# A two-layer decoder on one core: rows of split activations at other offsets and pitches, and products of weight groups in four orders

## The chip, the core and the metric

The kernel runs on one core of one Trainium2 chip. The metric is the device time of one execution in microseconds (us); less is better. A core has five engines with instruction queues of their own: TensorE (PE, matrix products; the load of the stationary weights is shown apart as PEld), VectorE (DVE), ScalarE (ACT), GpSimd (POOL) and SyncE (SP, used here to issue DMA transfers). They work on SBUF, a memory of 128 partitions; TensorE writes to PSUM, and VectorE and ScalarE read from there.

## The reference

A sequence of 16 learned prefix tokens and 256 input tokens (272 in all, model width 2048, 16 heads) goes through two layers. Layer 0 has attention with a forget gate, layer 1 stick-breaking attention against a K/V projection that is computed once. Each layer ends with an MLP that squares the positive part. Cut to what matters:

```python
def squared_relu_mlp(h, w_up, w_down):
    u = h @ w_up
    return jnp.square(jax.nn.relu(u)) @ w_down
...
        if layer < N_A_LAYERS:
            proj = a @ fox_w_in[i]
            q, k, v, f_logit = jnp.split(proj, [D_MODEL, 2 * D_MODEL, 3 * D_MODEL], axis=-1)
...
            o = forgetting_attention(split_heads(q), split_heads(k), split_heads(v), cum_logf)
            h = h + o.reshape(b, length, D_MODEL) @ fox_w_o[i]
        else:
            c = rms_norm(h, kv_norm)
            k_s, v_s = jnp.split(c @ w_kv, 2, axis=-1)
...
            q = split_heads(a @ sb_w_q[i])
            o = stick_breaking_attention(q, shared_k, shared_v)
            h = h + o.reshape(b, length, D_MODEL) @ sb_w_o[i]
        h = h + squared_relu_mlp(rms_norm(h, norm_mlp[layer]), w_up[layer], w_down[layer])
    return rms_norm(h, final_norm)[:, N_META:]
```

All of it is float32. The hidden width of the MLP is 8192.

## The kernel before

Activations are kept with features on the partitions: 16 chunks of 128 features, each with a row of 272 tokens (256 in layer 1, which needs no prefix queries). To have nearly float32 exactness at the rate of a shorter format, each operand x is split into a high part and a low part, both of the type float32r, and a product w·x is the sum of three: high·high, high·low and low·high.

**Rows.** The class `Split` holds one stage's activations. A tile has, for each of the 16 chunks, a row of XROW = 576 elements; the high half begins at element XHI = 16, the low half right behind it. `both` is the view over the two halves of a row together. Two such tiles exist and are used in turn (tag "x"). The stages and their labels: a0 (input of layer 0's q, k, v), o0 (attention output), m0 (input of the MLP), u0_0 to u0_3 (the four quarters of the MLP's hidden vector), a1 and kv (inputs of layer 1's q and of K/V), o1, m1, u1_0 to u1_3. The last one, `ob`, takes the output. The helpers `split_chunk`, `put_split` and the evacuation in `mlp` write the halves with ScalarE (high) and VectorE (low).

**Groups.** All projections go through `gemm_group`, one call for 512 output features. There are 96 calls, numbered by u = 1 to 96: 12 for q, k and v of layer 0 (a0), 4 on o0, 32 in its MLP (16 on m0, 4 on each of u0_0 to u0_3), 4 for q of layer 1 (a1), 8 for K/V (kv), 4 on o1 and 32 in the MLP (m1, u1_0 to u1_3). A call walks over the 2048 input features in four blocks kb of four chunks kc. For each block, two DMA transfers on SP's queue bring 512 KB each into tiles `raw` (ring of four), and each half is split: ScalarE writes `whi` (line 213), VectorE `wlo` (line 214), with rings of four tiles each, so two blocks are held. Four PSUM accumulators, m = 0 to 3, take 128 output features each.

**Order of the products.** Blocks 0 and 3 are walked output by output (m outside, all four chunks inside). Blocks 1 and 2 are walked in halves of two chunks, with all four m inside each. In layer 0 and for K/V a chunk and an m give three products of 272 columns, issued one behind the other: high weights × high half, high weights × low half, low weights × high half. In layer 1 (`pairs`) there are two: high weights × `both` (512 columns, so that the two sums stand side by side in PSUM) and low weights × high half (256 columns); in a run all products of the first kind go before those of the second. All are issued through the helper `gemm_matmul` (line 172), which pins each product behind the one before it, apart from the first group (`load_x`), where the planner of the framework may reorder. In block 3 the accumulator m is evacuated as soon as its products are issued.

Between groups, attention runs with its own products on TensorE; its exponentials and masks lie on ScalarE and VectorE beside the next group's products. `gate_products` multiplies the rows of a0 with a narrow weight block (32 columns) within the first group.

**Scratch.** `kernel` creates the program with the default size of the SBUF region kept for descriptors of dynamic DMA transfers.

## Time and profile before

| what | value |
|---|---|
| median of 2 runs | 2333.88 us (2332.91 to 2334.85) |
| profiled execution | 2332.09 us, span of its instructions 2330.3 us |
| PE busy | 2319.3 us, 16486 products |
| DVE, ACT, POOL busy | 1350.6, 1064.8 and 38.9 us |
| granted TensorE clock | 0.998 of full speed |
| read from HBM | 407.29 MB, 176 GB/s over the span |

The span is the time from the first to the last instruction of one profiled execution. Products on TensorE are pipelined: one starts while the one before it still drains, so the mean time of one product in a row of the profile is longer than the distance from its start to the next start. In a row of the table of groups stand the line, engine and operation, output <- inputs by the program's names, the shape of the stationary block and of the moving rows, the count, the busy time, the mean time of one in ns, and the idle time before with what ended it. In the timeline stand the start in us, the length of the merged stretch, and the same names.

### The profile page before, as it was taken

To read this page: it belongs to the slowest core of one execution; us is meant where nothing else is said; L and a number is where in the kernel's file an instruction comes from. 1 tells how busy PE (TensorE), PEld (TensorE's weight loads), DVE (VectorE), ACT (ScalarE), POOL (GpSimd) and SP (SyncE) were. 2 spreads that over 40 slices of the span, in tenths; PEclk is the share of its full clock that TensorE was granted. 3 is DMA by queue.
4 is the path that set the end of the run, shared out by engine and by line. 5 is a ranking of instruction groups with operands and counts; after the bars stand their busy time and mean duration, and the time that the engine had idled before them with its cause. 6 is when DMAs were issued, how large, how long until landed. Compare 5 with 4: busy or idle time off the path is not lost.

```text
span 2330.3 us, 39954 instructions
## 1 busy us (share of the span) xinstructions
PE 2319.3 (100%) x16486; PEld 2200.1 (94%) x16486; DVE 1350.6 (58%) x1923; ACT 1064.8 (46%) x1477; POOL 38.9 (2%) x58
## 2 busy tenths in 40 slices
PE   9999999999999999999999999999999999999998
PEld 9999999999999999999998999988888888888887
DVE  7665555654454455445566555566665665655665
ACT  6434344543344344334455444455543543543553
POOL 1000000000000000000000000000000000000000
PEclk9999999999999999999999999999999999999999
DMA  6544545455545555555556444446556556555553
GB/s 233 172 155 163 169 158 171 166 185 173 180 168 185 176 174 180 172 182 172 181 175 198 160 145 145 145 163 199 184 190 198 186 187 199 185 191 195 185 198 128
DMA packets 116630, 412.00 MB, mean 177 GB/s; under 512 B 13264, under 2 KB 16736, under 8 KB 116448
## 3 DMA queue, kind: packets, MB, share of 16 engines
q1 hardware_dynamic: 114560, 406.29, 52.4%
q10 hardware_dynamic: 1888, 3.16, 0.4%
q8 instruction: 129, 2.11, 0.4%
q14 instruction: 53, 0.43, 0.1%
HBM read 407.29 MB, written 2.11 MB: 176 GB/s over the span
## 4 chain that ended last, share of the span: by engine, by line
PE 99%; DVE 0%; ACT 0%; issue 0%; DVEq 0%; ACTq 0%
PE acc L172 96%; PE ps L402 0%; PE pza L581 0%; PE pv L335 0%; PE po L464 0%; PE po L620 0%; PE idle L60 0%; PE pzb L582 0%; PE po L621 0%; PE po L465 0%; PE po L622 0%; DVE ob L676 0%; PE pf L301 0%; PE pf L302 0%; PE pta L597 0%; PE pta L596 0%
## 5 line engine op out<-in xcount | busy, mean ns | idle before, releaser
L214 DVE TENSOR_TENSOR wlo<-raw,whi 128x1024 fp32r<-128x1024 f32 (+1 forms) x773 | 931.7, 1217 | 752.6 <-ACT whi L213 751.7
L213 ACT ACTIVATE whi<-raw 128x1024 fp32r<-128x1024 f32 (+1 forms) x773 | 799.2, 1050 | 960.4 <-PE acc L172 939.9
L172 PE MATMUL acc<-x_u,whi 128*128 128x272 f32 (+2 forms) x3088 | 650.8, 322 | 0.0
L172 PE MATMUL acc<-x_m,whi 128*128 128x272 f32 (+1 forms) x3072 | 649.2, 323 | 0.0
L172 PEld LDWEIGHTS acc<-x_u,whi 128*128 128x128 f32 x3088 | 497.4, 188 | 26.3
L172 PEld LDWEIGHTS acc<-x_m,whi 128*128 128x128 f32 x3072 | 495.5, 188 | 26.9
L172 PE MATMUL acc<-x_u,wlo 128*128 128x272 f32 (+1 forms) x2048 | 441.7, 280 | 0.0
L172 PE MATMUL acc<-x_m,wlo 128*128 128x272 f32 (+1 forms) x2048 | 439.4, 280 | 0.0
L172 PE MATMUL acc<-x_a,whi 128*128 128x272 f32 (+1 forms) x1792 | 363.0, 307 | 0.0
L172 PEld LDWEIGHTS acc<-x_u,wlo 128*128 128x128 f32 x2048 | 339.5, 188 | 15.9
L172 PEld LDWEIGHTS acc<-x_m,wlo 128*128 128x128 f32 x2048 | 338.5, 188 | 16.1
L172 PEld LDWEIGHTS acc<-x_a,whi 128*128 128x128 f32 x1792 | 283.5, 188 | 9.3 <-issue 0.7
L172 PE MATMUL acc<-x_a,wlo 128*128 128x272 f32 (+1 forms) x1024 | 252.9, 284 | 0.0
L172 PE MATMUL acc<-x_kv,whi 128*128 128x272 f32 x1024 | 195.8, 289 | 0.0
L172 PEld LDWEIGHTS acc<-x_a,wlo 128*128 128x128 f32 x1024 | 179.3, 188 | 4.7 <-issue 0.5
L172 PE MATMUL acc<-x_o,whi 128*128 128x272 f32 (+1 forms) x768 | 163.1, 323 | 0.0
L172 PEld LDWEIGHTS acc<-x_kv,whi 128*128 128x128 f32 x1024 | 159.9, 188 | 0.4
L172 PE MATMUL acc<-x_kv,wlo 128*128 128x272 f32 x512 | 145.9, 285 | 0.0
L252 DVE TENSOR_TENSOR hT<-acc,hT 128x256 f32<-128x256 f32 (+1 forms) x239 | 102.5, 429 | 72.0 <-PE acc L172 70.3
L172 PEld LDWEIGHTS acc<-x_o,whi 128*128 128x128 f32 x768 | 124.0, 188 | 6.7
L172 PE MATMUL acc<-x_o,wlo 128*128 128x272 f32 (+1 forms) x512 | 110.8, 282 | 0.0
L172 PEld LDWEIGHTS acc<-x_kv,wlo 128*128 128x128 f32 x512 | 96.2, 188 | 0.1
(226 smaller groups left out, 1038.5 us busy)
## 6 DMA issues: line engine op xcount, KB each, us to landing
raw<-w_up SPq DMA_DIRECT2D x256, 512.0 KB, 4.7
raw<-w_dn SPq DMA_DIRECT2D x256, 512.0 KB, 4.8
raw<-w_qkv SPq DMA_DIRECT2D x92, 512.0 KB, 4.1
raw<-w_o SPq DMA_DIRECT2D x64, 512.0 KB, 4.5
raw<-w_kv SPq DMA_DIRECT2D x64, 512.0 KB, 3.9
raw<-w_q SPq DMA_DIRECT2D x32, 512.0 KB, 4.7
fk<-f_dram ACTq DMA_DIRECT2D x4, 544.0 KB, 5.4
raw<-w_qkv SPq DMA_DIRECT2D x7, 256.0 KB, 4.7
```

What stands on the lines that cost most here:

```text
L172: ins = nc.tensor.matmul(*args, **kw).ins
L213: on_act = nc.scalar.activation(hp, src, AF.Copy)
L214: on_dve = nc.vector.tensor_tensor(out=lp, in0=src, in1=hp.bitcast(F32), op=ALU.subtract)
L252: nc.vector.tensor_tensor(out=hT[:, c, t0:], in0=a, in1=hT[:, c, t0:], op=ALU.add)
```

## The change

Three things change.

1. `Split` takes offset and pitch from a table `ROWS` by the stage's label: pitch of a row, start of the high half, start of the low half, in elements. The tile is 16 × 640 + 64 elements for every stage. In layer 1, where `both` is used, the low half still stands right behind the high half.
2. `gemm_group` chooses one of four orders by u modulo 4. The first group's first block and, for all groups, the order of m in blocks 0 and 3 stay as they are; within them, and in blocks 1 and 2, the products of a chunk and an m may be drawn apart. `kinds` lists the products (0 = high weights, 1 = low weights).
   - Without pairs: order 0 walks halves of two chunks, and in each all high × high, then all high × low, then all low × high; order 1 the same over the whole block; order 2 is the order of before; order 3 walks halves, and in each output by output the three kinds one after the other over its chunks.
   - With pairs: order 0 is the order of before; order 1 walks the whole block at once; order 2 halves, output by output; order 3 output by output over the whole block, as blocks 0 and 3.
3. The program keeps 1,024 bytes for descriptors of dynamic DMA transfers.

```diff
-XROW = 576
-XHI = 16
+ROWS = {"a0": (576, 16, 288), "kv": (640, 0, 320), "o0": (640, 16, 336), "m0": (640, 32, 352), "u0_0": (640, 48, 368),
+        "u0_1": (544, 0, 272), "u0_2": (576, 48, 320), "u0_3": (576, 0, 272),
+        "a1": (576, 0, 256), "o1": (576, 32, 288), "m1": (512, 0, 256), "u1_0": (576, 48, 304), "u1_1": (544, 16, 272),
+        "u1_2": (576, 0, 256), "u1_3": (576, 8, 264)}
+XROW = 640
...
-            rows = xs.tile([P, NC, XROW], F32R, tag="x", name=f"x_{label}")
-            self.hi, self.lo = rows[:, :, XHI:XHI + n], rows[:, :, XHI + n:XHI + 2 * n]
-            self.both = rows[:, :, XHI:XHI + 2 * n]
+            rows = xs.tile([P, NC * XROW + 64], F32R, tag="x", name=f"x_{label}")
+            pitch, hi, lo = ROWS[label]
+            rows = rows[:, hi:hi + NC * pitch].rearrange("p (c t) -> p c t", c=NC)
+            self.hi, self.lo = rows[:, :, :n], rows[:, :, lo - hi:lo - hi + n]
+            self.both = rows[:, :, :2 * n] if lo == hi + n else None
...
+            way = u % 4
             if load_x is not None and kb == 0:
                 runs = [([kc], range(4)) for kc in range(4)]
-            elif kb in (0, 3):
+            elif kb in (0, 3) or way == 3 and pairs:
                 runs = [(range(4), [m]) for m in range(4)]
+            elif way == 1:
+                runs = [(range(4), range(4))]
+            elif way == 2 and pairs:
+                runs = [(range(2 * hf, 2 * hf + 2), [m]) for hf in range(2) for m in range(4)]
             else:
                 runs = [(range(2 * hf, 2 * hf + 2), range(4)) for hf in range(2)]
             pinned[0] = load_x is None
             for kcs, ms in runs:
                 paired = [m for m in ms if pairs and m not in apart]
...
+                for some in (paired, [m for m in ms if m not in paired]):
+
+                    kinds = ([(0, sp.both, 2 * n), (1, sp.hi, n)] if some is paired else
+                             [(0, sp.hi, n), (0, sp.lo, n), (1, sp.hi, n)])
+                    if not pairs and way == 2:
+                        todo = [(i, kc, m) for m in some for kc in kcs for i in range(len(kinds))]
+                    elif not pairs and way == 3:
+                        todo = [(i, kc, m) for m in some for i in range(len(kinds)) for kc in kcs]
+                    else:
+                        todo = [(i, kc, m) for i in range(len(kinds)) for kc in kcs for m in some]
+                    for i, kc, m in todo:
+                        w, xk, cols = kinds[i]
+                        gemm_matmul(accs[m][:, :cols], parts[kc // 2][w][:, kc % 2, m * P:(m + 1) * P],
+                                    xk[:, 4 * kb + kc], start=kb == kc == i == 0,
+                                    stop=kb == kc == 3 and i == len(kinds) - 1)
...
-    ob = xs.tile([P, NC, XROW], F32, tag="x", name="ob")
+    ob = xs.tile([P, NC * XROW + 64], F32, tag="x", name="ob")[:, :NC * XROW].rearrange("p (c t) -> p c t", c=NC)
...
-    nc = bacc.Bacc("TRN2", target_bir_lowering=False, num_devices=1)
+    nc = bacc.Bacc("TRN2", target_bir_lowering=False, num_devices=1, dynamic_dma_scratch_size=1024)
```

More of the change, by code (lines that the diff above doesn't have):

```diff
@@ L229, in gemm_group @@
                 paired = [m for m in ms if pairs and m not in apart]
-                single = [m for m in ms if m not in paired]
-                for kc in kcs:
-                    for m in paired:
-                        gemm_matmul(accs[m], parts[kc // 2][0][:, kc % 2, m * P:(m + 1) * P], sp.both[:, 4 * kb + kc],
-                                    start=kb == kc == 0, stop=False)
-                for kc in kcs:
-                    for m in paired:
-                        gemm_matmul(accs[m][:, :n], parts[kc // 2][1][:, kc % 2, m * P:(m + 1) * P],
-                                    sp.hi[:, 4 * kb + kc], start=False, stop=kb == kc == 3)
-                for m in single:
-                    for kc in kcs:
-                        wh, wl = (w[:, kc % 2, m * P:(m + 1) * P] for w in parts[kc // 2])
-                        hi, lo = sp.hi[:, 4 * kb + kc], sp.lo[:, 4 * kb + kc]
-                        gemm_matmul(accs[m][:, :n], wh, hi, start=kb == kc == 0, stop=False)
-                        gemm_matmul(accs[m][:, :n], wh, lo, start=False, stop=False)
-                        gemm_matmul(accs[m][:, :n], wl, hi, start=False, stop=kb == kc == 3)
+                for some in (paired, [m for m in ms if m not in paired]):
[12 more added lines that the diff above has]
+                                    stop=kb == kc == 3 and i == len(kinds) - 1)
                 if kb == 3:
```

## The prediction, made before the result was known

> **What bounds the kernel now.** I read the page first: shares, granted clock, chain, costliest groups.

> ```profile
> span 2330.3 us, 39954 instructions
> ...
> PE 2319.3 (100%) x16486; PEld 2200.1 (94%) x16486; DVE 1350.6 (58%) x1923; ACT 1064.8 (46%) x1477; POOL 38.9 (2%) x58
> ...
> PEclk9999999999999999999999999999999999999999
> ...
> PE 99%; DVE 0%; ACT 0%; issue 0%; DVEq 0%; ACTq 0%
> PE acc L172 96%; PE ps L402 0%; PE pza L581 0%; PE pv L335 0%; PE po L464 0%; PE po L620 0%; PE idle L60 0%; PE pzb L582 0%; PE po L621 0%; PE po L465 0%; PE po L622 0%; DVE ob L676 0%; PE pf L301 0%; PE pf L302 0%; PE pta L597 0%; PE pta L596 0%
> ...
> L214 DVE TENSOR_TENSOR wlo<-raw,whi 128x1024 fp32r<-128x1024 f32 (+1 forms) x773 | 931.7, 1217 | 752.6 <-ACT whi L213 751.7
> L213 ACT ACTIVATE whi<-raw 128x1024 fp32r<-128x1024 f32 (+1 forms) x773 | 799.2, 1050 | 960.4 <-PE acc L172 939.9
> ```

> TensorE runs from end to end at the full granted clock, and 96% of the chain is the one helper line that issues the products of the groups. ScalarE, which splits the weights, stands idle for 940 us because TensorE has not yet freed a weight tile: the weights are early, not late. Next I asked what TensorE itself waits for. The whole answer is three rows, 2.6 us in all:

> ```profile
> PE pr_fin L665 <- DVE fin L659: 1.3, 1, 1.3
> PE idle L60 <- DVE mean_w L56: 1.1, 1, 1.1
> PE pms_fin L633 <- ACT sq_fin L645: 0.2, 1, 0.2
> ```

> So the time is the number of products times the distance between their starts, and the change keeps the number. Only that distance can move it. Third view: TensorE's groups by shape (count, union of their spans, mean time of one).

> ```profile
> L172 PE MATMUL acc<-x_m,whi 128*128 128x272 f32 x2048 | 382.7, 288 | 0.0
> ...
> L172 PE MATMUL acc<-x_u,wlo 128*128 128x272 f32 x1024 | 289.8, 283 | 0.0
> L172 PE MATMUL acc<-x_m,whi 128*128 128x512 f32 x1024 | 266.5, 392 | 0.0
> ...
> L172 PE MATMUL acc<-x_m,wlo 128*128 128x256 f32 x1024 | 149.5, 278 | 0.0
> ...
> L598 PE MATMUL pta<-eh,nones_r 128*128 128x288 f32 x8 | 2.4, 296 | 0.0
> ```

> Products overlap, so a mean is longer than the distance. The distances come from the timeline of TensorE; first an MLP stage of layer 0 (start, time, what, count):

> ```profile
> 600.13 0.41 PE L172 MATMUL acc<-x_u,whi 128*128 128x272 f32 x2
> 600.38 0.28 PE L172 MATMUL acc<-x_u,wlo 128*128 128x272 f32 x1
> ...
> 603.86 0.41 PE L172 MATMUL acc<-x_u,whi 128*128 128x272 f32 x2
> ```

> From 600.13 to 603.86 there are ten triples (high x high, high x low, low x high): 373 ns a triple, 124.4 ns a product. Within one, the two products with high weights take some 126 ns each (0.25 us, rounded) and the third 121. Set against the means 288 and 283, a mean is the distance plus 162 ns; I use that below for groups whose starts I do not quote. In layer 1, where a product runs over both halves of a row (512 columns) or over the high half (256):

> ```profile
> 1711.78 2.00 PE L172 MATMUL acc<-x_u,whi 128*128 128x512 f32 x8
> 1713.62 1.07 PE L172 MATMUL acc<-x_u,wlo 128*128 128x256 f32 x8
> 1714.52 1.07 PE L172 MATMUL acc<-x_u,whi 128*128 128x512 f32 x4
> 1715.44 0.63 PE L172 MATMUL acc<-x_u,wlo 128*128 128x256 f32 x4
> 1715.91 1.09 PE L172 MATMUL acc<-x_u,whi 128*128 128x512 f32 x4
> 1716.84 0.62 PE L172 MATMUL acc<-x_u,wlo 128*128 128x256 f32 x4
> 1717.29 1.07 PE L172 MATMUL acc<-x_u,whi 128*128 128x512 f32 x4
> ```

> Runs of like products do not all go alike: 512 columns take 230, 230 and 232.5 ns, 256 columns 112.5, 117.5 and 112.5. The means 392 and 278 less 162 give 230 and 116 for a whole stage, 346 ns a pair. The ten equal triples above cross chunk boundaries and different output blocks, so the stretch is a regular property of the stream, not a disturbance by other engines.

> By the loops there are 56 groups of 192 products in layer 0 and the K/V stage (10,752) and 40 of 64 pairs in layer 1 (2,560): 10,752 x 124.4 ns = 1,338 us and 2,560 x 346 ns = 886 us, 2,224 of 2,330 us. One ns on every product of the first kind is 10.8 us; one ns on every pair is 2.6 us.

> [...]

> **Part by part.** *Order of the products.* Group u takes order u modulo 4, so a stage of four groups has each order once. Without pairs, order 2 is the old order; 0, 1 and 3 run the products in like runs. With pairs, order 0 is the old one; the others lengthen or shorten the runs in the two middle weight blocks. The first group, whose order is not pinned, already runs in like runs:

> ```profile
> 10.29 1.17 PE L172 MATMUL acc<-x_a,whi 128*128 128x272 f32 x8
> 11.30 0.67 PE L172 MATMUL acc<-x_a,wlo 128*128 128x272 f32 x4
> 11.80 1.17 PE L172 MATMUL acc<-x_a,whi 128*128 128x272 f32 x8
> ```

> Twelve products in 1.51 us: 125.8 ns. A neighbouring dozen differs by 0.01 us, so I take 125.4, 1.0 ns above the old order. Three quarters of 10,752 are 8,064 products: +8.1 us. Bounds: the best like run above, 112.5 ns for 256 columns, is 120 for 272, which also is the third product of a triple; the worst is the 126.3 of the first two. So -4 to +2 ns, -32 to +16 us. In layer 1 the old stream holds both kinds of run: 8 and 8 products, (1.84 + 0.90) / 8 = 342 ns a pair (its neighbour is longer), and 4 and 4, (0.92 + 0.47) / 4 and (0.93 + 0.45) / 4, 346. The orders move half of the blocks of some groups between these: 30 groups x 32 pairs x at most 4 ns = 4 us either way; I take +0.4.

> *Offset and pitch of the rows.* Here the trace can say less. The old pitch is 2,304 bytes, nine times 256, so in every chunk the high half starts 64 and the low half 128 bytes past a multiple of 256 (tiles are whole multiples of 256 long, before and after). These two offsets cost the same to within 1 ns: the first two products of a triple. The new table uses 0, 32, 64, 128 and 192. Two groups of rows tell what other reads cost. L598 reads 288 columns in two pieces of another tile: 296 - 162 = 134 ns, where 288 columns at the rate of the triples would be 131.7: +2.3. And the gate products, whose weight block is only 32 columns wide (128*32):

> ```profile
> 30.96 0.29 PE L302 MATMUL pf<-x_a,wf 128*32 128x272 f32 x1
> ...
> 33.69 0.29 PE L302 MATMUL pf<-x_a,wf 128*32 128x272 f32 x1
> ```

> That is 22 distances in 2.73 us, 124.1 ns: as long as with full blocks. The stretch thus hangs on reading the row, not on how long the weight load is, and so an offset could move it. Bounds for layer 0: the 120 and the +2.3 above, -4.4 to +2.3 ns, -47 to +25 us. I take 0, by the nearest row, the two offsets that agree. For layer 1: best runs 230 + 112.5 against the mean 346, -3.5; worst 232.5 + 117.5, +4, and two offsets that L598 would charge, +4.6: -9 to +12 us. Its old mean lies nearer the good end, so a redraw costs a little; I take +1.5 ns a pair, +4 us.

> [...]

> *Weight tiles held longer.* In order 1 (and order 3 with pairs) a middle block reads both halves of its weights to the end, so the first half is freed half a block later, 24 products or 3 us. ScalarE's next split, VectorE's behind it, and the load on SP's queue that waits for the raw tile all shift by that. The ring holds two blocks, so a full block (48 x 124.4 ns = 6.0 us; 16 x 346 ns = 5.5 us in layer 1) remains for two splits of 1,050 ns and one of 1,217 behind them, 3.3 us. 2 us are over, hidden under the other block's products: 0. Without that cover it would be up to 3 us in 24 groups, 72 us; the 940 us of idle ScalarE say that it is there.

> *Start.* Only in the first group are weights just in time, and its second and third block now sweep all four chunks before they use low weights: they ask for the second half after 8 products, not after 24. Bounds 0 to 2 x 2 us; I take +1.5.

> *Rest.* The splits write as many elements as before; the larger tiles and the scratch cost no instruction, and the profile's list of DMA queues has none that software fills: 0.

> Sum: 8.1 + 0.4 + 0 + 4 + 1.5 = +14 us on the profiled execution's 2,332.1 (span 2,330.3 and 1.8 around it), 2,346. The median shown lies 1.8 us above that execution: **2,348 us**.

> **Rivals.** *Slower: rows that start where weight blocks start.* Weight blocks are 512 bytes and begin at multiples of 256. Rows at offset 0 would begin in step with them: in layer 0 and K/V all of kv (1,536 products), the high half of u0_3 (512), the low half of u0_2 (256), every second chunk of u0_1's high half (256); in layer 1 a1, m1 and u1_2 (3,072): 5,632 products. If each pays two steps of the size seen between runs (117.5 - 112.5 = 5 ns), that is 56 us: 2,348 + 56 = **2,404**. It decides from (47 - 14) / 5,632 = 6 ns each. For it: runs do lock into slower and faster patterns. Against it: 64 and 128 cost alike, and the gate rows. Chance 0.18.

> *Faster: the clean pattern everywhere.* All products at 120 ns and pairs at 230 + 112.5: -47 - 9 + 1.5, **2,279**. For it: such runs exist. Against it: it needs nearly all of 60 combinations of layout and order to hit, while four orders in turn average. Chance 0.08.

> [...] Chance 0.16.

> **Numbers.** My forecast has 0.58. Two per cent is 47 us, about what a measurement of this kernel can tell from no change: 0.08 faster, 0.58 + 0.16 = 0.74 within, 0.18 slower. The forecast's own range: the bounds of the order and offset terms, shrunk because some 60 combinations average, some 25 us either way. To leave out no more than 2 in 10 the range goes most of the way to both outer rivals: 2,300 to 2,392.

> **What would show it.** Mean less 162 ns, by stage: near 125 (272 columns), 230 to 232 and 116 to 118. If kv, m1 and u1_2 stand out by over 6 ns, the first rival holds; if all stages are near 120, the second. Between groups of one stage, order 2 of layer 0 should be the quickest by 1 ns a product. TensorE's waits should stay near 3 us with ScalarE still idle on TensorE; a wait of products for weight tiles would prove the cover wrong. The first group should end 1 to 2 us later. A drop of the granted clock would make the prediction wrong altogether.

## The result and the profile after

| kernel | median us | runs | ratio to before (95% interval) |
|---|---|---|---|
| before | 2333.88 | 2 | |
| changed | 2357.52 | 2 | 1.0101 (1.0058 to 1.0145) |
| changed, once more beside the experiments | 2358.16 | 4 | 1.0105 (1.0092 to 1.0119) |

The changed kernel is slower by 24 us, 1.0%. The prediction was 2,348 us, +14 us. From the page of the changed kernel, its parts in the order in which those of before were shown (the helper's line is now 178, the splits are lines 219 and 220):

```profile
span 2355.3 us, 39966 instructions
...
PE 2344.4 (100%) x16486; PEld 2220.0 (94%) x16486; DVE 1343.7 (57%) x1923; ACT 1062.7 (45%) x1477; POOL 39.8 (2%) x58
...
PEclk9999999999999999999999999999999999999999
...
L220 DVE TENSOR_TENSOR wlo<-raw,whi 128x1024 fp32r<-128x1024 f32 (+1 forms) x773 | 924.7, 1217 | 759.8 <-ACT whi L219 710.6
L219 ACT ACTIVATE whi<-raw 128x1024 fp32r<-128x1024 f32 (+1 forms) x773 | 794.9, 1051 | 973.2 <-PE acc L178 943.5
```

The same 16,486 products, the same granted clock (0.998), TensorE again busy from end to end, ScalarE again idle for 943 us on TensorE. What TensorE waits for, the whole answer:

```profile
PE pr_fin L675 <- DVE fin L669: 1.3, 1, 1.3
PE idle L64 <- DVE mean_w L60: 1.1, 1, 1.1
PE pms_fin L643 <- ACT sq_fin L655: 0.2, 1, 0.2
PE acc L178 <- ACT whi L219: 0.2, 1, 0.2
```

There is one new wait, of 0.2 us. So the 25 us more of span are time between the starts of products. Two stages of layer 0 in the changed kernel, both in the old order of products (order 2), show where: m0, whose halves start at 128 bytes past a multiple of 256, and u0_0, where both start at 192 (timeline of TensorE: start, length, what, count).

```profile
468.07 0.29 PE L178 MATMUL acc<-x_m,wlo 128*128 128x272 f32 x1
...
474.15 0.29 PE L178 MATMUL acc<-x_m,wlo 128*128 128x272 f32 x1
...
564.55 0.29 PE L178 MATMUL acc<-x_u,wlo 128*128 128x272 f32 x1
...
570.47 0.29 PE L178 MATMUL acc<-x_u,wlo 128*128 128x272 f32 x1
```

Sixteen triples lie between the two rows of each stage: 6.08 us / 48 = 126.7 ns a product in m0, 5.92 / 48 = 123.3 in u0_0. Before, both stages ran at 124.4. Taken so from the starts of all products (medians of the groups of a stage; in layer 0 and K/V ns a product, in layer 1 ns a pair; halves in bytes modulo 256):

| stage | halves, changed | before | changed: order 0, 1, 2, 3 | stage's length, change in us |
|---|---|---|---|---|
| a0 | 64, 128 | 124.7 | 126.2, 126.3, 124.7, 125.6 | +3.2, 1.3 of it in the first group |
| o0 | 64, 64 | 124.4 | 126.7, 126.6, 126.7, 126.7 | +1.7 |
| m0 | 128, 128 | 124.4 | 126.7, 126.6, 126.7, 126.7 | +6.8 (four times) |
| u0_0 | 192, 192 | 124.4 | 123.3, 123.4, 123.3, 123.3 | -0.9 |
| u0_1, u0_2, u0_3 | 0 or 128 and 64 or 192; 192, 0; 0, 64 | 124.4 | 124.4 to 125.8 | +0.8, +0.2, +0.7 |
| kv | 0, 0 | 124.5 | 125.3 to 125.5 | +1.2 |
| a1 | 0 | 346.3 | 350.0, 349, 349.5, 350.8 | +0.9 |
| o1 | 128 | 345.2 | 351.2, 351, 350.1, 351.0 | +1.4 |
| m1 | 0 | 345.2 | 350.0, 349, 349.5, 350.8 | +4.8 (four times) |
| u1_0 | 192 | 345.2 | 346.7, 347.0, 346.7, 346.7 | +0.4 |
| u1_1, u1_2, u1_3 | 64 or 192; 0; 32 | 345.2 | 348.3 to 350.9 | +1.0, +1.2, +0.9 |

(In order 1, a1, o1 and m1 have attention's products in between; their figures there are good to about 1 ns.) The stages of layer 0 behind a0, with K/V, are 10.5 us longer, layer 1 is 10.5 longer, the orders in a0 cost 2 and the start 1.3: 24 of 25. The run with the rows alone, below, has the same two sums, 10.7 and 10.5, so they belong to the offsets. In layer 0, where both halves of every row start alike at 64, 128 or 192 (o0, m0, u0_0), the order moves the distance by 0.1 ns at most; in a0, where they do not, by 1.6. In layer 1 the two halves always start alike, and there the order still moves a pair by 1 to 2 ns (m1: 349 to 350.8).

### The profile page after: what moved, and what is told of

It reads as the page before. It is cut to its first block, busy times and chain, and to the rows that moved or that the text cites. A ratio compares the mean times of both kernels' runs of the same rounds, so it can differ in the third digit from the quotient of the medians.

```text
span 2355.3 us, 39966 instructions
## 1 busy us (share of the span) xinstructions
PE 2344.4 (100%) x16486; PEld 2220.0 (94%) x16486; DVE 1343.7 (57%) x1923; ACT 1062.7 (45%) x1477; POOL 39.8 (2%) x58
## 4 chain that ended last, share of the span: by engine, by line
PE 99%; DMA 0%; ACT 0%; DVE 0%; issue 0%; DVEq 0%; SPq 0%; ACTq 0%
PE acc L178 95%; PE ps L412 0%; PE pza L591 0%; PE pv L345 0%; PE po L474 0%; PE po L630 0%; DMA raw<-w_qkv 0%; PE pzb L592 0%; PE po L631 0%; PE po L475 0%; DMA hT<-hT_in 0%; PE po L632 0%; ACT whi L219 0%; DVE ob L686 0%; PE pf L312 0%; PE pf L311 0%
## 5 line engine op out<-in xcount | busy, mean ns | idle before, releaser
L220 DVE TENSOR_TENSOR wlo<-raw,whi 128x1024 fp32r<-128x1024 f32 (+1 forms) x773 | 924.7, 1217 | 759.8 <-ACT whi L219 710.6
L178 PE MATMUL acc<-x_m,whi 128*128 128x272 f32 (+1 forms) x3072 | 599.6, 325 | 0.0
L178 PE MATMUL acc<-x_u,whi 128*128 128x272 f32 (+2 forms) x3088 | 595.8, 322 | 0.0
L178 PEld LDWEIGHTS acc<-x_m,whi 128*128 128x128 f32 x3072 | 462.0, 188 | 23.5
L178 PEld LDWEIGHTS acc<-x_u,whi 128*128 128x128 f32 x3088 | 459.3, 188 | 22.8
L178 PE MATMUL acc<-x_m,wlo 128*128 128x272 f32 (+1 forms) x2048 | 362.8, 285 | 0.0
L178 PE MATMUL acc<-x_u,wlo 128*128 128x272 f32 (+1 forms) x2048 | 360.0, 283 | 0.0
L178 PE MATMUL acc<-x_a,whi 128*128 128x272 f32 (+1 forms) x1792 | 321.3, 307 | 0.2 <-ACT whi L219 0.2
L178 PE MATMUL acc<-x_a,wlo 128*128 128x272 f32 (+1 forms) x1024 | 193.1, 288 | 0.0
L178 PE MATMUL acc<-x_kv,wlo 128*128 128x272 f32 x512 | 100.3, 288 | 0.0
L508 ACT ACTIVATE u<-relu 128x272 f32<-128x272 f32 (+1 forms) x128 | 54.3, 424 | 73.0 <-DVE relu L506 72.8
```

The costliest lines, as they stand in the source:

```text
L178: ins = nc.tensor.matmul(*args, **kw).ins
L220: on_dve = nc.vector.tensor_tensor(out=lp, in0=src, in1=hp.bitcast(F32), op=ALU.subtract)
L508: nc.scalar.activation(u2[:, t0:], r[:, t0:], AF.Square)
```

## The experiments

The theory after the result ("offsets"): the distance of the products follows from where the two halves of a row start modulo 256 bytes, and the order counts only where they start differently. Rivals: the orders cost it all; or the larger tiles and the smaller scratch, which move everything else in SBUF, do.

**The orders alone.** The changed kernel's `gemm_group`, with

```diff
-            pitch, hi, lo = ROWS[label]
...
+            self.hi, self.lo = rows[:, :, XHI:XHI + n], rows[:, :, XHI + n:XHI + 2 * n]
+            self.both = rows[:, :, XHI:XHI + 2 * n]
```

and XROW = 576, XHI = 16, tiles and scratch as before.

> The four orders alone: rows, tiles and scratch as before. Theory 'offsets' (the distance of products follows from where the two halves of a row start, modulo 256 bytes; the order counts only where the halves start differently): all rows here start at 64 and 128 bytes, as a0 does in the changed kernel, where orders 0, 1 and 3 cost 126.2, 126.3 and 125.6 ns against 124.4 and order 2 costs nothing. 14 groups of each order x 192 products x (1.8 + 1.9 + 0 + 1.2) ns = 13 us; in layer 1 nothing to speak of: 2347 us. Rival 'orders' (the whole loss comes from the orders, in all stages): 2357 us. Rival 'room' (the larger tiles and the smaller scratch move what else lies in SBUF): 2334 us.

Measured: 2347.82 us, ratio 1.0059 (1.0047 to 1.0072), +14 us. Every stage of layer 0 now shows what a0 showed: 126.2, 126.3, 124.4 and 125.6 ns for orders 0, 1, 2, 3. In m0, a group of order 0, from its first row to its last:

```profile
510.03 1.17 PE L173 MATMUL acc<-x_m,whi 128*128 128x272 f32 x8
...
533.76 0.67 PE L173 MATMUL acc<-x_m,wlo 128*128 128x272 f32 x4
```

188 products lie between the two starts: 23.73 us / 188 = 126.2 ns.

**The rows alone.** The changed kernel with the loops of before in `gemm_group`.

> Rows, tiles and scratch of the changed kernel, products in the old order. Theory 'offsets': stages as in the changed kernel (m0 and o0 at 126.7 ns, u0_0 at 123.3, kv at 125.3, layer 1 at 347 to 351 ns a pair), only a0 falls back to 124.4: 2 to 3 us less than the changed kernel, 2355 us. Rival 'orders': 2334 us. Rival 'room': 2357 us.

Measured: 2353.90 us, ratio 1.0086 (1.0072 to 1.0100), +20 us. The two parts alone come to 14 + 20 = 34 us, not 24: with the new rows the orders cost 4 us (2353.90 to 2358.16), about 2 of it in a0 and most of the rest at the start.

**The room alone.** All stages at (576, 16, 288), in layer 1 (576, 16, 272), old order, new tiles and scratch.

> The larger tiles and the scratch of 1,024 bytes alone: every row at the old offset and pitch, products in the old order. Theory 'offsets' and rival 'orders': the same as before, 2334 us, 124.4 ns a product and 345 ns a pair. Rival 'room': 2357 us.

Measured: 2333.16 us, ratio 0.9998 (0.9989 to 1.0007). The room costs nothing.

**Both halves at 192.** Old order, all stages of layer 0 and kv at (640, 48, 368), all of layer 1 at (576, 16, 272):

```diff
-        "a0": (576, 16, 288), "kv": (640, 0, 320)
+        "a0": (640, 48, 368), "kv": (640, 48, 368)
...
-        "a1": (576, 0, 256), "o1": (576, 32, 288)
+        "a1": (576, 16, 272), "o1": (576, 16, 272)
```

> Old order; all rows of layer 0 and of K/V with both halves at 192 bytes (pitch 640, as u0_0 in the changed kernel), rows of layer 1 as before. Theory 'offsets': 123.3 ns in all 56 groups, -1.1 ns x 10,752 = -12 us: 2322 us, faster than both kernels. If the pattern belongs to u0_0's place in the program and not to its rows, 2334 us.

Measured: 2323.68 us, ratio 0.9956 (0.9944 to 0.9969): faster than before by 10 us and than the changed kernel by 34. From its timeline, an MLP stage of layer 0:

```profile
599.94 0.28 PE L175 MATMUL acc<-x_u,wlo 128*128 128x272 f32 x1
...
603.64 0.28 PE L175 MATMUL acc<-x_u,wlo 128*128 128x272 f32 x1
```

Ten triples in 3.70 us, 123.3 ns, in all stages. Layer 1, whose rows are those of before, gave 1 ns a pair back: 346.4 in all its stages, where before a1 ran at 346.4 and the others at 345.2.

**Which address is it?** The kernel before with the weight tiles 64 bytes higher, and the rows at the same addresses as before:

```diff
-XHI = 16
+XHI = 0
...
-    pad = align.tile([P, 32], F32, name="pad")
+    pad = align.tile([P, 48], F32, name="pad")
```

> The kernel before with the weight tiles moved 64 bytes up, and the rows left where they were (64 and 128 past a multiple of 256; the tiles move 64 bytes, the offset within them falls by 64). Theory 'rows alone' (only the row's own address counts): 124.4 ns and 345 ns a pair, 2334 us. Rival 'distance' (what counts is how far the row starts behind the weight block that is loaded beside it): the halves now stand 0 and 64 behind the weights, as u0_3 does with the old order (125.8 ns), and layer 1 stands at 0, as a1, m1 and u1_2 do (350 ns a pair): 10,752 x 1.4 + 2,560 x 4.5 ns = 27 us more, 2361 us.

Measured: 2358.91 us (one execution) beside 2332.87 for before, +26 us. No row has moved, and the whole of it goes as if the rows had: 125.8 ns where u0_3 in the old order had 125.8, and 350.0 a pair. Two blocks of a stage of layer 1, first the changed kernel (m1, rows at 0, weights at 0, old order), then this one (rows at 64, weights at 64):

```profile
1692.83 1.09 PE L178 MATMUL acc<-x_m,whi 128*128 128x512 f32 x4
1693.76 0.63 PE L178 MATMUL acc<-x_m,wlo 128*128 128x256 f32 x4
1694.23 1.09 PE L178 MATMUL acc<-x_m,whi 128*128 128x512 f32 x4
1695.15 0.64 PE L178 MATMUL acc<-x_m,wlo 128*128 128x256 f32 x4
...
1698.44 2.00 PE L178 MATMUL acc<-x_m,whi 128*128 128x512 f32 x8
```

```profile
1648.62 1.09 PE L172 MATMUL acc<-x_m,whi 128*128 128x512 f32 x4
1649.55 0.63 PE L172 MATMUL acc<-x_m,wlo 128*128 128x256 f32 x4
1650.02 1.09 PE L172 MATMUL acc<-x_m,whi 128*128 128x512 f32 x4
1650.95 0.64 PE L172 MATMUL acc<-x_m,wlo 128*128 128x256 f32 x4
...
1654.23 0.40 PE L172 MATMUL acc<-x_m,whi 128*128 128x512 f32 x1
```

**Other pairs of offsets.** Old order, one untried pair in each stage.

> Old order, another untried pair of offsets in each stage (bytes past a multiple of 256, high and low half): a0 0 and 128, o0 0 and 192, m0 64 and 0, u0_0 64 and 192, u0_1 128 and 0, u0_2 128 and 64, u0_3 192 and 64, kv 192 and 128; in layer 1 a1 16, o1 48, m1 80, u1_0 96, u1_1 160, u1_2 224, u1_3 240. If a half's start alone set its own product's distance, layer 0 would follow from the equal pairs, (2 x high half + low half) / 3 of 125.3, 126.7, 126.7 and 123.3 for 0, 64, 128, 192: a0 125.8, o0 124.6, m0 126.2, u0_0 125.6, u0_1 126.2, u0_2 126.7, u0_3 124.4, kv 124.4. If the two starts work together, as 64 and 128 did before (124.4 where this sum says 126.7), some stage falls below 123.3. In layer 1 offsets within the same 64 bytes should go like 0, 64, 128 or 192 below them if only lines of 64 bytes count: 350, 350, 345, 345, 351, 347, 347.

Measured (one execution): 2353.23 us. Layer 0: a0 125.1, o0 128.9, m0 125.2, u0_0 124.4, u0_1 124.4, u0_2 125.9, u0_3 124.4, kv 124.6; layer 1: 348.3, 350.4, 350.4, 353.3, 351.7, 351.2, 350.4. The additive rule fails by up to 4 ns (o0), so the two starts work together; the expectation had some stage fall below 123.3 in that case, and none did. In layer 1, 80 and 96 bytes (350.4 and 353.3) are not as good as 64 (345.2): the position within 64 bytes counts too.

**The curve by itself, and the length of the weight load.**

> The faster kernel (both halves at 192 bytes) with a measurement put in front of it: 28 series of 32 products of constant data, each series with one moving row at a fixed offset (probe a to p: 0, 16, ... 240 bytes past a multiple of 256, 272 columns) against weight blocks of 128 columns that start at multiples of 256; then 512 columns (wide), 256 columns (half) and, for 272 columns, weight blocks of 32 columns (slim) at 0, 64, 128, 192. The time as a whole grows by the series, some 110 us, and is not compared. The profile's mean of a group less 162 ns is the distance. Theory 'distance to the weight block': 272 columns at 0, 64, 128, 192 go as kv, o0, m0, u0_0 did: 125.3, 126.7, 126.7, 123.3 ns; off the 64 byte grid 125 to 129. [...] Rival 'the collision is at the start of the load': slim series as the full ones, 123 to 127 ns, and as the gate products before (124.1).

From the timeline of the series with 256 columns (half) and with weight blocks of 32 columns (slim); a, e, i, m stand for 0, 64, 128, 192:

```profile
99.07 3.99 PE L129 MATMUL probeahalf<-probe,wprobe 128*128 128x256 f32 x32
102.90 3.93 PE L129 MATMUL probeehalf<-probe,wprobe 128*128 128x256 f32 x32
106.67 3.95 PE L129 MATMUL probeihalf<-probe,wprobe 128*128 128x256 f32 x32
110.46 3.79 PE L129 MATMUL probemhalf<-probe,wprobe 128*128 128x256 f32 x32
114.09 4.21 PE L129 MATMUL probeaslim<-probe,wprobe 128*32 128x272 f32 x32
118.13 4.12 PE L129 MATMUL probeeslim<-probe,wprobe 128*32 128x272 f32 x32
122.09 4.14 PE L129 MATMUL probeislim<-probe,wprobe 128*32 128x272 f32 x32
126.06 4.16 PE L129 MATMUL probemslim<-probe,wprobe 128*32 128x272 f32 x32
130.06 0.42 PE L198 MATMUL acc<-x_a,whi 128*128 128x272 f32 x2
```

Start to start, divided by 32: 120, 118, 118 and 113 ns for 256 columns; 126, 124, 124 and 125 for 272 columns beside the short load. The full series of 272 columns ran between 123.3 and 126.7 at all sixteen offsets, at 0, 64, 128 and 192 as the stages did (125.2, 126.7, 126.6, 123.3); 512 columns at 226.8, 229.0, 232.4 and 233.4. So a load of a quarter of the width moves the pattern, 2 to 3 ns down at 64 and 128 and over 1 up at 0 and 192, but brings none below 123.8. The range is the rival's.

**Can layer 1 take the best of both?** By these series 512 columns want distance 0 and 256 columns 192. The low weights of layer 1 were moved 64 bytes up, its rows to 0:

```diff
-                wlo = wspl.tile([P, 2, 512], F32R, tag="wlo", name=f"wlo_{u}_{kb}_{hf}")
+                w0 = 16 if pairs else 0
+                wlo = wspl.tile([P, 1088], F32R, tag="wlo", name=f"wlo_{u}_{kb}_{hf}")
+                wlo = wlo[:, w0:w0 + 1024].rearrange("p (k c) -> p k c", k=2)
```

> The faster kernel with layer 1 set by the series of the measurement: rows at 0, where 512 columns beside high weights went at 226.8 ns, and the low weights of layer 1 moved 64 bytes up, so that the 256 columns stand 192 behind them, where they went at 113.3 ns. Old order. If each product follows the distance to its own weights and settles at once: 340 ns a pair against 346.4, 2,560 x 6.3 ns = 16 us less than the faster kernel's 2323.7 (both halves at 192): 2308 us. If the change from one kind of run to the other costs what it gained, no gain: 2320 to 2326 us. If what counts is the distance to the high weights alone, the low products stay at 119.9 ns, as half at 0 did: 347 ns a pair, 2325 us.

> As the one before, but layer 1 walks the middle blocks in runs of 16 products of a kind, not 8. If only changes of kind cost, it gains on it by up to half of what that kernel falls short of 340 ns a pair; if runs settle at once, the same time within 2 us.

Measured: 2329.43 us, ratio 0.9985 (0.9977 to 0.9994), and 2328.29, ratio 0.9979 (0.9970 to 0.9988); both are slower than the kernel with both halves at 192 alone, 348.8 and 348.1 ns a pair. None of the three expectations of the first holds. The longer runs of the second gained 1.1 us. That is within the 2 us that its expectation had for runs that settle at once, but the starts show that they do not. Its timeline:

```profile
1626.73 3.82 PE L175 MATMUL acc<-x_m,whi 128*128 128x512 f32 x16
1630.38 2.05 PE L175 MATMUL acc<-x_m,wlo 128*128 128x256 f32 x16
1632.27 3.82 PE L175 MATMUL acc<-x_m,whi 128*128 128x512 f32 x16
```

Sixteen long products take 3.65 us, 228 each (by the starts, the first five 229 to 236 ns, then steadily 226 to 227, as the series). The low ones take 1.89 us, 118 each from the first to the last, neither 113 nor 120. So a run settles only after some products, and may settle on another pattern than the one that the series showed.

**All triples.**

> The faster kernel with 64 series of 12 triples in front (high x high, high x low, low x high; 272 columns; constant data): high half, low half and low weights each 0, 64, 128 or 192 past a multiple of 256 (letters a, e, i, m in this order), high weights at 0. The time as a whole grows by some 290 us and is not compared. Means less 162 ns should repeat the stages: aaa 125.3, eea 126.7, iia 126.7, mma 123.3, eia 124.4, aea 125.8, maa 124.4. [...]

Measured from the starts: between 123.3 (high half 192, low half 192, low weights 0 gives 123.3; 64, 128, 64 gives 123.4) and 126.7 ns; the other 62 series lie at 124.3 or above. The seven series that repeat a stage came as the stages did: aaa 125.6, eea 126.7, iia 126.5, mma 123.3, eia 124.4, aea 125.7, maa 124.4. No other series beats both halves at 192 with the low weights at 0. The place of the low weights alone moves a triple too: mma 123.3, mme 126.7, mmi 124.4, mmm 125.5.

**The theory used to forecast.** The changed kernel with two entries exchanged:

```diff
-        "m0": (640, 32, 352)
+        "m0": (640, 48, 368)
...
-        "m1": (512, 0, 256)
+        "m1": (576, 16, 272)
```

> The changed kernel itself, again, for a narrower interval: 2357 to 2358 us, ratio 1.010.

> The changed kernel with two stages' rows exchanged: m0 at 192 and 192 (was 128 and 128), m1 at 64 (was 0). Theory: m0's 16 groups go from 126.7 to 123.3 ns, -10.4 us; m1's 16 groups from 350 to 345 or 346.4 ns a pair (both patterns were seen at 64), -4 to -5 us; all other stages stay. 2342 to 2343 us. If a stage's pattern hangs on what the stages before it did, others move too and the sum is off by more than 3 us.

Measured: 2358.16 us and 2342.61 us, ratio 1.0039 (1.0025 to 1.0053): 15.6 us less, as forecast. m0 went to 123.3, m1 to 345.2 to 346.3, and no other stage moved by more than 0.3. From m0 in the second kernel, order 2:

```profile
465.94 0.29 PE L178 MATMUL acc<-x_m,wlo 128*128 128x272 f32 x1
...
471.86 0.29 PE L178 MATMUL acc<-x_m,wlo 128*128 128x272 f32 x1
```

Sixteen triples take 5.92 us here; with the rows at 128 they took 6.08.

## Why the prediction was right, and where its sum was not

That the change would cost time, and about how much, came right in part by luck. The largest term, the orders, was forecast at 8.5 us in all and is 2 in this kernel; the two terms of the offsets were forecast at 4 and are 21. The errors have opposite signs, and the sum fell 10 us short.

**What bounds the kernel** was right: nothing but the distance between products moved; clock, count, waits and the idle of ScalarE stayed.

**Weight tiles held longer, and the rest**, costed at nothing: right. No wait for weights appears outside the first group, and the room alone measured 0.9998.

**The start**, +1.5 us: it is +1.3 (the second group begins at 35.1 us, before at 33.8, 0.1 of it from a later first product), and 1.8 to 2.0 in the three other kept executions with the new orders. The cause is the one named, the second half of a block's weights asked for early: the stream of the second block stalls behind its eighth product.

```profile
12.14 2.02 PE L178 MATMUL acc<-x_a,whi 128*128 128x272 f32 x12
14.32 2.80 PE L178 MATMUL acc<-x_a,whi 128*128 128x272 f32 x20 [0.16 <-ACT whi L219]
16.96 2.19 PE L178 MATMUL acc<-x_a,wlo 128*128 128x272 f32 x16
```

Thirty-two products take 4.82 us here, where at 126 ns they would take 4.0; one wait, 0.16 us for `whi`, stands in the profile by name.

**The orders**, +8.1 us by the first group's like runs: the row was read rightly (125.4 to 125.8 ns there; 126.2, 126.3 and 125.6 on the chip with the old rows) and the mechanism exists. With the old rows it costs more than forecast, 14 us with the start; in the changed kernel nearly all that is left of it is a0's 2 us, and only there is order 2 the quickest by 1 ns (in u0_3 it is the dearest, 125.8). The step that failed took the orders and the offsets as two terms to be added. They are one thing: the order decides which starts follow each other, and where all starts of a layer-0 stage are alike it changes nothing that the starts show.

**Offsets in layer 0**, 0 us, measured +10.5. This is the step that failed most: "I take 0, by the nearest row, the two offsets that agree". That 64 and 128 cost alike within one triple said nothing on rows that start at 64 twice, or at 128 twice: those run at 126.7, both. The bounds (-47 to +25 us) held.

**Offsets in layer 1**, +4 us, measured +10.5, at the dear end of the bounds (-9 to +12). The direction and its reason ("its old mean lies nearer the good end") were right: the old rows' 64 is the best start for a pair that any run found.

**What the stretch hangs on.** "On reading the row, not on how long the weight load is" is half right. The short loads measured by themselves shift the pattern by offset, but bring no offset below 123.8. And the weights' address does as much as the row's: 64 bytes on the weight tiles alone cost 26 us. From a load's length the prediction had concluded on the load as a whole.

**The rivals.** The slower one named the right mechanism, the start of the row against the start of the weight blocks, but wrong places and prices: at 0 a product of 272 columns costs 1 ns more than before (kv), not 10, while 64 with 64 and 128 with 128, which it held harmless, cost 2.3; in layer 1, 0 costs 4.8 ns a pair. The faster one was refuted: no triple runs at 120, the best is 123.3. The outcome with the chance 0.16, 2,335 us with the start's term alone and nothing done to the stream, was refuted by every stage but u0_2.

**The rough tool.** "A mean is the distance plus 162 ns" is good to 2 ns only: means of 286 to 287 belong to 123.3 in the faster kernel and 290 to 126.7 in m0 of the changed one, where the rule gives 124 to 125 and 128. Starts in the timeline are what to divide.

What stays open: what makes the stretch (no run shows that two reads collide), and whether it is the load for the next product or the product's own block that sets it. The patterns' dependence on their past was seen, not explained.

## What to carry to other kernels

Where TensorE streams float32r products without a wait, time a product from starts in the timeline and compare stages: 1% can lie in where rows start behind the weight blocks, and a padding of some elements moves it either way. Such an offset, the offset of the weights and the order of products are to be tuned together, not added up; a layout in which all rows of a stage start alike made the order of the triples in layer 0 indifferent, though not that of the pairs in layer 1. A factorial test inside one kernel (a layout for each stage, an order for each group) is cheap to read, since the profile gives every stage its own distance.

## What the runs showed of the hardware beyond that

- The distances are exact and repeat: m0 ran at 126.6 or 126.7 ns in all of its 16 groups, and again in a second execution of the changed kernel, while ScalarE, VectorE and the DMA transfers went on beside them.
- The same offsets of rows and weights and the same order can settle on two patterns: layer 1 at 64 ran at 346.4 ns a pair in a1 and at 345.2 from o1 on before, and at 346.4 throughout in the kernel with layer 0 at 192.
- The best series had 123.3 ns for 272 columns, 226.8 for 512 and 113.3 for 256. At the rate of those 256 columns 272 would take 120.4, an estimate from the 113.3 alone; no series or stage of 272 columns came to it.
- The rate behind the split into two parts of float32r stands in the profile of before. A plain float32 product of 256 columns (`pza`, L581, 16 products) has two records there, and from each to the next start there are 216 ns (320 between the two in 4 of the 16): 432 a product. The float32r products that replace one, a pair of 512 and 256 columns in layer 1, take 346.
